# A two-layer hybrid backbone: where the low part of u is formed, and where the latent gates' modulation sums are taken

## The chip, the core and the metric

The kernel runs on one core of a Trainium2 chip. The metric is the device time of one execution in microseconds. The core's engines are TensorE (PE, matrix products; PEld is its weight load), VectorE (DVE), ScalarE (ACT), GpSimd (POOL) and SyncE (SP, which issues nearly all transfers here). Each engine works through its own queue in order; they meet through semaphores. TensorE reads SBUF and writes PSUM; VectorE and ScalarE read both.

## The reference, cut to what matters

```python
def conformer_conv(va, vg, p):
    u = va * jax.nn.sigmoid(vg)
    u = depthwise_conv(u, p["conv_w"], p["conv_b"], CONV_PAD)        # 31 taps
    return jax.nn.silu(layernorm(u, p["ln_g"], p["ln_b"]))

def rglru_branch(xb, p, h0, with_outputs):
    u = depthwise_conv(xb, p["sconv_w"], p["sconv_b"], SHORT_CONV_PAD)   # 4 taps
    # gates r, i = sigmoid(per-head products of u); a = exp(-8 r softplus(-lam))
    # b = sqrt(1 - a^2) * i * u; scan h = a h + b forward and backward
    ...

def even_mixer(h, h0, p):
    va, vg, ga, xb, gb = jnp.split(h @ p["w_in"], ...)
    y_a = conformer_conv(va, vg, p) * jax.nn.silu(ga)
    y_b = rglru_branch(xb, p, h0, True) * jax.nn.silu(gb)
    return jnp.concatenate([y_a, y_b], axis=-1) @ p["w_out"]

# layer: shift, scale, gate = split(silu(c) @ mod_w + mod_b, 3)
#        x = x + gate * mixer(rmsnorm(x) * (1 + scale) + shift)
# layer 0 is even_mixer; layer 1 is a pooling mixer; a final rmsnorm follows.
```

There are 1024 latent tokens and 256 context tokens of width 1024. The context passes only through the RG-LRU branch and gives the states with which the latent scans start.

## The kernel before

All values are kept transposed: 128 features on the partitions, tokens along the free dimension. A 1024-wide operand is `KT = 8` tiles. Products are made in three passes: each operand is split into a high part rounded to fp32r (a cast on ScalarE, L95) and a low part (the difference, on VectorE or GpSimd, L96), and high·high, high·low and low·high are added in PSUM (L126 to L128, and L508 to L510 for the gates).

The first stage, to about 90 us, loads x and the context, takes the modulation's sums for shift and scale, normalises, and folds weights of the second layer. A modulation sum (`mod_tile`, L212 and L216) multiplies a 128 x 1024 tile of weights by the vector silu(c) and adds along the row.

Then come eight rounds, j = 0 to 7, one for each 128 features of both branches. In round j:

- `uc` is the short convolution of `xb` (ScalarE L531, VectorE L534), `uh` and `ul` its high and low part. `ul` is made by `split` on VectorE as soon as `uc` and `uh` are there.
- `decays(j-1)` turns the gates of the round before into the scan's factors, on ScalarE (L449, a chain kept in order, with three changes of the activation table).
- The products `vg` (sigmoid on ScalarE, `sg`) and `va` follow; `u = va * sg` is made in two halves on VectorE (L564, called `va_0` and `va_1` here), with raised priority.
- `recurrence(j-1)`: GpSimd multiplies (L463, then a pair L465, one for each direction), VectorE multiplies (L468), scans the context (L475) and the latents (L477) for each direction, and adds both (L480).
- `project_xb(j+1)` makes the next round's `xb`, and the gate products of round j (`gate_steps`) are woven into it. The first pass of a gate product needs `uh`, the second `ul`.

In the last round there is no next `xb`; the gate products are woven into `va`. The 31 taps of the long convolution (L739, one tensor in PSUM, one in SBUF) run on VectorE whenever it is free, through the rounds and after them. GpSimd also makes the low parts of the weights (`wl_xb`, `wl_gw` and so on), and adds the layer norm's sums (`lnsum`, L748 and L751).

After the rounds come the products `gb` (silu on ScalarE L719, multiplied with the scan's result on VectorE L720, split again) and `wob` (taken out of PSUM by VectorE L789 with the latent gate `m0`), the layer norm (`mu`, `ms_ln`), `ga`, the rest of layer 0, and layer 1. Before the `gb` products the eight modulation sums of the latent gate (tiles 16 to 23) are loaded and taken, two for each of the first four `gb` steps, from a freshly loaded copy `cG` of silu(c).

The order of the work on each engine is set by a scheduler: it simulates the program as written, with priorities (`tc.high_priority`) and explicit orders (`tc.issue_after`), and writes one fixed queue for each engine. PSUM tiles of products come from four buffers in turn (`pm`): in a round they are `vg_0`, `vg_1`, `va_0`, `va_1`, the context part of the next `xb`, and then the gate groups, so that the second gate group takes the buffer of `va_0` and the third that of `va_1`. Wide tiles of a round (`utile`, `ltile`) come from pools of four and six buffers.

Of the kernel before, what the change touches and what calls it, by code (L numbers as in the profile page):

```python
# [15 lines left out]
P = 128  # L16
# [39 lines left out]
def body(ctx, tc, xT, ctxT, cc, ccol, modT, modW, win, gw, wout, wu, grp, wg, wo1, small, edge, ident, outT):  # L56
# [37 lines left out]
    def split(src, hi, lo, eng):  # L94
        return (nc.scalar.copy(hi, src),  # L95
                eng.tensor_tensor(out=lo, in0=src, in1=hi.bitcast(F32), op=sub))  # L96
# [12 lines left out]
    def wload(src, name, eng, n=D, out=None):  # L109
        raw = wpool.tile([P, n], F32, tag="wr", name=f"wr_{name}")  # L110
        load(raw, src)
        if out is None:
            hi = wpool.tile([P, n], F32R, tag="wh", name=f"wh_{name}")
            lo = wpool.tile([P, n], F32R, tag="wl", name=f"wl_{name}")
        else:
            hi, lo = out(f"wh_{name}", F32R), out(f"wl_{name}", F32R)
        split(raw, hi, lo, eng)
        return hi, lo
# [311 lines left out]
    with ExitStack() as actx:  # L430
# [84 lines left out]
        def weave(some, others, n):  # L515
            for _ in some:
                for _ in range(n):
                    next(others, None)
            for _ in others:
                pass  # L520
# [5 lines left out]
        for j in range(KT):  # L526
            uc = utile(f"uc{j}")

            for src, dst in zip(xb, (uc[:, :C], uc[:, C:])):
                n = src.shape[-1]  # L530
                nc.scalar.activation(dst, src, AF.Identity, bias=col(O_SCB + j), scale=col(O_SCW + 4 * j + 2))  # L531
                for k, o in ((0, -2), (1, -1), (3, 1)):
                    a, b = max(0, -o), n - max(0, o)
                    nc.vector.scalar_tensor_tensor(out=dst[:, a:b], in0=src[:, a + o : b + o],  # L534
                                                   scalar=col(O_SCW + 4 * j + k), in1=dst[:, a:b],
                                                   op0=mult, op1=add)
            uh, ul = utile(f"uh{j}", F32R), utile(f"ul{j}", F32R)
            split(uc, uh, ul, nc.vector)

            roots, root = (None, None) if state is None else decays(j - 1, state[1])  # L540
            w = wload(win[KT + j], f"vg{j}", nc.gpsimd)
            sg = []
            for h in range(2):
                ps = psum(f"vg{j}_{h}")
                mm3(ps, w, (hh, hl), HALF[h])
                t = ttile(f"sg{j}_{h}")
                with ExitStack() as octx:
                    if root is not None:
                        octx.enter_context(tc.issue_after(root.ins))
                    octx.enter_context(tc.high_priority(offset=EVAC))  # L550
                    nc.scalar.activation(t, ps, AF.Sigmoid)
                sg.append(t)
            w = wload(win[j], f"va{j}", nc.gpsimd)
            u = xtile(f"u{j}")
            us.append(u)
            gates, last = [], j == KT - 1
            gate = lambda: gate_steps(j, wload(gw[j], f"gw{j}", nc.gpsimd, n=4 * P), (uh, ul), gates)

            def value_steps():
                for h in range(2):  # L560
                    ps = psum(f"va{j}_{h}")
                    yield from mm3_steps(ps, w, (hh, hl), HALF[h])
                    with tc.high_priority(offset=EVAC):
                        nc.vector.tensor_tensor(out=u[:, HALF[h]], in0=ps, in1=sg[h], op=mult)  # L564

            weave(gate() if last else (), value_steps(), 1)
            if state is not None:
                recurrence(j - 1, *state, roots)
            if not last:
                xb, steps = project_xb(j + 1)  # L570
                weave(gate(), steps, 2)
            state = uc, gates
        recurrence(KT - 1, *state, decays(KT - 1, state[1])[0])

# [4 lines left out]
    def d2tile(name, dt=F32):  # L579
        return d2pool.tile([P, S], dt, tag="d2", name=name)  # L580
# [120 lines left out]


    bh, bl = [], []
    cG = d2tile("cG")
    load_c(0, cG)
    for j in range(KT):
        for m in range(2 * KT + 2 * j, min(2 * KT + 2 * j + 2, 3 * KT)):
            raw = d2tile(f"mod0_{m}")
            nc.sync.dma_start(raw, modT[0, m])
            mod_tile(m0, 0, m, raw, (cG,), raw)  # L710
        w = wload(win[4 * KT + j], f"gb{j}", nc.gpsimd)
        th, tl = d2tile(f"ybh{j}", F32R), d2tile(f"ybl{j}", F32R)
        for h in range(2):
            ps = psum(f"gb{j}_{h}")
            mm3(ps, w, (hh, hl), HALF[h])
            y = vtile(f"yr{j}_{h}")
            nc.sync.dma_start(y, yb_raw[j][:, HALF[h]])
            sgt = ttile(f"sb{j}_{h}")
            nc.scalar.activation(sgt, ps, AF.Silu)  # L719
            nc.vector.tensor_tensor(out=y, in0=y, in1=sgt, op=mult)  # L720
            split(y, th[:, HALF[h]], tl[:, HALF[h]], nc.gpsimd)
        bh.append(th)
        bl.append(tl)
# [701 lines left out]
```

## Time and profile before

| | |
|---|---|
| median of 3 runs (lowest to highest) | 1399.46 us (1398.16 to 1401.67) |
| the profiled execution: its time, its span | 1398.43 us, 1396.7 us |
| busy: TensorE, VectorE, ScalarE, GpSimd | 1299.7, 1192.6, 635.9, 362.3 us |
| mean granted TensorE clock | 0.97 |
| first stage; rounds 1 to 6; last round | to 92; 148 to 444; 444 to 484 us |
| `gb` and `wob`; `ga`; the rest | 484 to 678; 678 to 766; 766 to 1397 us |

Busy time of one engine lies beside that of others, so it is no sum. What can be gained is the time in which the engine that sets the end of a stage stands still, and that is read from that stage's waits. In rows of instructions the columns are: start, duration, engine, line, operation, tiles written and read, shape, count, and in brackets the idle time before and what ended it. In rows of waits they are: who, for whom, us in total, times, longest.

### The profile page before, as it was taken

The numbers are of one execution on the slowest core, as the hardware profiler recorded it, in microseconds if no ns is written. First come the engines' busy times: TensorE is split into PE (matmuls) and PEld (weight loads), VectorE is DVE, ScalarE is ACT, GpSimd is POOL, SyncE is SP. The second block draws the span as 40 slices with busy tenths as digits, with TensorE's granted clock in tenths as the row PEclk, the third lists the DMA queues.
The fourth block names the chain that finished last, engine by engine and source line by source line (L and its number), as shares of the span: only waits on it lengthen the run. The fifth ranks groups of instructions, "written<-read, shape, count | busy, mean of one in ns | idle before, by whom it ended". The sixth has DMA issues, their size and how long they took to land.

```text
span 1396.7 us, 15641 instructions
## 1 busy us (share of the span) xinstructions
PE 1299.7 (93%) x5664; PEld 1053.0 (75%) x5664; DVE 1192.6 (85%) x1587; ACT 635.9 (46%) x909; POOL 362.3 (26%) x182
## 2 busy tenths in 40 slices
PE   7889989898899799989999899999999999999895
PEld 4468877787777587868888688788878888778684
DVE  7984898999889999988888974999989987876675
ACT  6353653664474542311643544654333434634442
POOL 5182633652464453522521004100000000000002
PEclk9999999999999899999999999999999999999998
DMA  9741111111102116343344636523334334757623
GB/s 358 269 136 39 45 46 46 53 39 60 53 23 77 46 52 241 106 153 126 127 139 167 211 121 203 159 83 134 137 121 143 114 112 130 263 189 271 203 106 121
DMA packets 83010, 182.32 MB, mean 131 GB/s; under 512 B 7794, under 2 KB 27634, under 8 KB 82932
## 3 DMA queue, kind: packets, MB, share of 16 engines
q1 hardware_dynamic: 74484, 177.12, 36.7%
q10 hardware_dynamic: 8448, 4.20, 1.0%
q8 instruction: 44, 0.72, 0.2%
q14 instruction: 34, 0.28, 0.1%
HBM read 137.25 MB, written 44.04 MB: 130 GB/s over the span
## 4 chain that ended last, share of the span: by engine, by line
PE 53%; DVE 29%; DMA 6%; issue 6%; ACT 4%; POOL 1%; SPq 0%; DVEq 0%; POOLq 0%; ACTq 0%
DVE conv L739 7%; DVE g L468 2%; DVE g L477 2%; PE wob L126 2%; PE wob L128 2%; PE wob L127 2%; DVE junk L212 1%; PE fold L251 1%; PE vg L126 1%; PE vg L128 1%; PE fold L250 1%; DMA yr_t<-y_t 1%; PE xb L126 1%; PE xb L127 1%; PE fold L249 1%
## 5 line engine op out<-in xcount | busy, mean ns | idle before, releaser
L739 DVE SCALAR_TENSOR_TENSOR conv<-u,sm,conv 128x1021 f32<-128x1021 f32 (+14 forms) x232 | 292.1, 1272 | 6.5 <-ACT conv L731 3.8
L1245 POOL TENSOR_TENSOR o<-x,rr 128x256 f32<-128x256 f32 (+1 forms) x9 | 8.3, 942 | 462.5 <-ACT rr L1233 460.3
L511 ACT ACTIVATE g<-g,sm 128x512 f32<-128x512 f32 (+1 forms) x96 | 58.7, 617 | 126.5 <-PE g L510 124.3
L463 POOL TENSOR_TENSOR g<-g,uc 128x1280 f32<-128x1280 f32 x16 | 48.3, 3017 | 125.0 <-ACT g L511 78.9
L96 POOL TENSOR_TENSOR wl_wu<-wr_wu,wh_wu 128x1024 fp32r<-128x1024 f32 x16 | 38.7, 2421 | 153.6 <-ACT wh_wu L95 148.2
L508 PE MATMUL g<-uh,wh_gw 128*128 128x512 f32 (+1 forms) x96 | 37.0, 386 | 29.5 <-DVE u L564 22.2
L249 PE MATMUL fold<-gh,wh_wu 128*128 128x512 f32 x128 | 52.5, 411 | 4.6 <-ACT wh_wu L95 4.6
L126 PE MATMUL wob<-ybh,wh_wob 128*128 128x512 f32 x128 | 51.2, 404 | 5.0 <-DVE xp L789 4.9
L250 PE MATMUL fold<-gl,wh_wu 128*128 128x512 f32 x128 | 51.7, 404 | 3.7 <-DVE gl L96 3.7
L128 PE MATMUL xb<-h0h,wl_xb 128*128 128x512 f32 x128 | 50.8, 396 | 4.2 <-POOL wl_xb L96 4.2
L126 PE MATMUL gb<-h0h,wh_gb 128*128 128x512 f32 x128 | 51.4, 402 | 3.4 <-ACT sb L719 3.3
L251 PE MATMUL fold<-gh,wl_wu 128*128 128x512 f32 x128 | 51.2, 409 | 2.7 <-POOL wl_wu L96 2.7
L128 PE MATMUL gb<-h0h,wl_gb 128*128 128x512 f32 x128 | 50.9, 399 | 1.6 <-POOL wl_gb L96 1.6
L126 PE MATMUL va<-h0h,wh_va 128*128 128x512 f32 x128 | 50.6, 396 | 0.8 <-ACT g L511 0.8
L126 PE MATMUL vg<-h0h,wh_vg 128*128 128x512 f32 x128 | 50.5, 395 | 0.8
L465 POOL TENSOR_TENSOR g<-g,th 128x1280 f32<-128x1280 f32 x16 | 46.9, 2953 | 16.8 <-ACT th L449 16.8
L127 PE MATMUL wob<-ybl,wh_wob 128*128 128x512 f32 x128 | 50.9, 401 | 0.0
L126 PE MATMUL xb<-h0h,wh_xb 128*128 128x512 f32 x128 | 50.9, 398 | 0.0
L127 PE MATMUL gb<-h0l,wh_gb 128*128 128x512 f32 x128 | 50.9, 397 | 0.0
L127 PE MATMUL xb<-h0l,wh_xb 128*128 128x512 f32 x128 | 50.7, 396 | 0.0
L128 PE MATMUL wob<-ybh,wl_wob 128*128 128x512 f32 x128 | 50.7, 401 | 0.0
L127 PE MATMUL va<-h0l,wh_va 128*128 128x512 f32 x128 | 50.4, 394 | 0.0
(551 smaller groups left out, 4297.9 us busy)
## 6 DMA issues: line engine op xcount, KB each, us to landing
mod<-modT SPq DMA_DIRECT2D x28, 512.0 KB, 5.9
wr_wu<-wu SPq DMA_DIRECT2D x16, 512.0 KB, 4.2
x_part<-xp SPq DMA_DIRECT2D x32, 256.0 KB, 2.4
mod<-modT SPq DMA_DIRECT2D x32, 256.0 KB, 3.4
wr_v<-wfold SPq DMA_DIRECT2D x16, 512.0 KB, 3.6
wr_g<-wg SPq DMA_DIRECT2D x16, 512.0 KB, 4.8
wr_wo<-wo SPq DMA_DIRECT2D x16, 512.0 KB, 4.4
yr_t<-y_t SPq DMA_DIRECT2D x16, 512.0 KB, 6.4
```

The lines of the kernel that those rows point to most:

```text
L96: eng.tensor_tensor(out=lo, in0=src, in1=hi.bitcast(F32), op=sub))
L126: nc.tensor.matmul(ps, hi[:, kc], xh[k][:, cols], start=(k == 0), stop=False)
L127: nc.tensor.matmul(ps, hi[:, kc], xl[k][:, cols], start=False, stop=False)
L128: nc.tensor.matmul(ps, lo[:, kc], xh[k][:, cols], start=False, stop=(k == ks - 1))
L249: nc.tensor.matmul(ps, wh[:, kc], gh[i], start=(i == 0), stop=False)
L250: nc.tensor.matmul(ps, wh[:, kc], gl[i], start=False, stop=False)
L251: nc.tensor.matmul(ps, wl[:, kc], gh[i], start=False, stop=(i == 3))
L463: nc.gpsimd.tensor_tensor(out=ius[d], in0=ius[d], in1=uc, op=mult)
L465: nc.gpsimd.tensor_tensor(out=ius[d], in0=ius[d], in1=roots[d], op=mult)
L508: nc.tensor.matmul(ps[:, :n], gwh[:, kc], uh[:, a : a + n], start=True, stop=False)
L511: nc.scalar.activation(t[:, a : a + n], ps[:, :n], AF.Sigmoid, bias=col(ob + d * KT + j))
L739: nc.vector.scalar_tensor_tensor(out=(us[j] if k == 30 else acp)[:, a:b], in0=us[j][:, a + o : b + o], scalar=col(O_CONVW + 31 * j + k), i ...
```

## The change

`ul` is no longer made by `split` in front of the round's products. In rounds 0 to 6 it is issued after the first value product has been multiplied out; in round 7 it is issued ahead of the woven `va` and gate products. The eight modulation sums of the latent gate move to round 0; they use the vector `cL`, which is still there from the first stage, and the wide buffers of the rounds, and the load and SiLU of `cG` go. The gate weights of the last round are requested in a statement ahead of `ul` and the value's steps.

```diff
             uh, ul = utile(f"uh{j}", F32R), utile(f"ul{j}", F32R)
-            split(uc, uh, ul, nc.vector)
+            nc.scalar.copy(uh, uc)
+            taken = []
...
-            gate = lambda: gate_steps(j, wload(gw[j], f"gw{j}", nc.gpsimd, n=4 * P), (uh, ul), gates)
 
             def value_steps():
                 for h in range(2):
                     ps = psum(f"va{j}_{h}")
                     yield from mm3_steps(ps, w, (hh, hl), HALF[h])
                     with tc.high_priority(offset=EVAC):
-                        nc.vector.tensor_tensor(out=u[:, HALF[h]], in0=ps, in1=sg[h], op=mult)
-
-            weave(gate() if last else (), value_steps(), 1)
+                        taken.append(nc.vector.tensor_tensor(out=u[:, HALF[h]], in0=ps, in1=sg[h], op=mult))
+
+            gws = wload(gw[j], f"gw{j}", nc.gpsimd, n=4 * P) if last else None
+            with ExitStack() as octx:
+                if not last:
+                    weave((), value_steps(), 1)
+                    octx.enter_context(tc.issue_after(taken[0].ins))
+                nc.vector.tensor_tensor(out=ul, in0=uc, in1=uh.bitcast(F32), op=sub)
+            if last:
+                weave(gate_steps(j, gws, (uh, ul), gates), value_steps(), 1)
+            if j == 0:
+                for m in range(2 * KT, 3 * KT):
+                    raw = ltile(f"mod0_{m}")[:, :D]
+                    nc.sync.dma_start(raw, modT[0, m])
+                    mod_tile(m0, 0, m, raw, (cL,), raw)
             if state is not None:
                 recurrence(j - 1, *state, roots)
             if not last:
                 xb, steps = project_xb(j + 1)
-                weave(gate(), steps, 2)
+                gws = wload(gw[j], f"gw{j}", nc.gpsimd, n=4 * P)
+                weave(gate_steps(j, gws, (uh, ul), gates), steps, 2)
...
     bh, bl = [], []
-    cG = d2tile("cG")
-    load_c(0, cG)
     for j in range(KT):
-        for m in range(2 * KT + 2 * j, min(2 * KT + 2 * j + 2, 3 * KT)):
-            raw = d2tile(f"mod0_{m}")
-            nc.sync.dma_start(raw, modT[0, m])
-            mod_tile(m0, 0, m, raw, (cG,), raw)
         w = wload(win[4 * KT + j], f"gb{j}", nc.gpsimd)
```

What the scheduler makes of it is seen in the queues. VectorE in round 1, before (`g_0_1` and `g_1_1` are the scan's inputs of the two directions, `conv` rows are taps of the long convolution, the two L564 rows are `va_0` and `va_1`):

```order
L96 TENSOR_TENSOR ul_1191<-uc_1181,uh_1190 128x1280
...
L468 SCALAR_TENSOR_TENSOR g_0_1_1079<-g_0_0_1045,g_0_1_1079 128x1280
...
L468 SCALAR_TENSOR_TENSOR g_1_1_1147<-g_1_0_1113,g_1_1_1147 128x1280
L564 TENSOR_TENSOR u_1268<-va_0_1269,sg_0_1233 128x512
L475 SCALAR_TENSOR_TENSOR g_0_1_1079<-g_0_0_1045,g_0_1_1079 128x256
L739 SCALAR_TENSOR_TENSOR conv_3862<-u_978,sm,conv_3862 128x1017
L475 SCALAR_TENSOR_TENSOR g_1_1_1147<-g_1_0_1113,g_1_1_1147 128x256
L477 SCALAR_TENSOR_TENSOR g_0_1_1079<-g_0_0_1045,g_0_1_1079 128x1024
L739 SCALAR_TENSOR_TENSOR conv_3862<-u_978,sm,conv_3862 128x1016
L477 SCALAR_TENSOR_TENSOR g_1_1_1147<-g_1_0_1113,g_1_1_1147 128x1024
L564 TENSOR_TENSOR u_1268<-va_1_1295,sg_1_1260 128x512
```

The same place now:

```order
L468 SCALAR_TENSOR_TENSOR g_0_1_1111<-g_0_0_1077,g_0_1_1111 128x1280
L746 SCALAR_TENSOR_TENSOR conv_3859<-u_977,sm,conv_3859 128x1018
L475 SCALAR_TENSOR_TENSOR g_0_1_1111<-g_0_0_1077,g_0_1_1111 128x256
L468 SCALAR_TENSOR_TENSOR g_1_1_1179<-g_1_0_1145,g_1_1_1179 128x1280
L564 TENSOR_TENSOR u_1299<-va_0_1300,sg_0_1264 128x512
L571 TENSOR_TENSOR ul_1223<-uc_1213,uh_1222 128x1280
L746 SCALAR_TENSOR_TENSOR conv_3859<-u_977,sm,conv_3859 128x1017
L477 SCALAR_TENSOR_TENSOR g_0_1_1111<-g_0_0_1077,g_0_1_1111 128x1024
L475 SCALAR_TENSOR_TENSOR g_1_1_1179<-g_1_0_1145,g_1_1_1179 128x256
L746 SCALAR_TENSOR_TENSOR conv_3859<-u_977,sm,conv_3859 128x1016
L564 TENSOR_TENSOR u_1299<-va_1_1326,sg_1_1291 128x512
```

`ul` has moved from the front to just behind `va_0`, and the second direction's long scan (L477) from ahead of `va_1` to behind it. (Taps have line 746 in the changed kernel.)

VectorE in round 3, before:

```order
L96 TENSOR_TENSOR ul_1795<-uc_1785,uh_1794 128x1280
L745 COPY u_1268<-conv_3895 128x15
L468 SCALAR_TENSOR_TENSOR g_0_1_1683<-g_0_0_1649,g_0_1_1683 128x1280
L739 SCALAR_TENSOR_TENSOR conv_3930<-u_1570,sm,conv_3930 128x1009
L475 SCALAR_TENSOR_TENSOR g_0_1_1683<-g_0_0_1649,g_0_1_1683 128x256
L468 SCALAR_TENSOR_TENSOR g_1_1_1751<-g_1_0_1717,g_1_1_1751 128x1280
L564 TENSOR_TENSOR u_1872<-va_0_1873,sg_0_1837 128x512
L739 SCALAR_TENSOR_TENSOR conv_3930<-u_1570,sm,conv_3930 128x1010
L477 SCALAR_TENSOR_TENSOR g_0_1_1683<-g_0_0_1649,g_0_1_1683 128x1024
L475 SCALAR_TENSOR_TENSOR g_1_1_1751<-g_1_0_1717,g_1_1_1751 128x256
L739 SCALAR_TENSOR_TENSOR conv_3930<-u_1570,sm,conv_3930 128x1011
L564 TENSOR_TENSOR u_1872<-va_1_1899,sg_1_1864 128x512
```

And now:

```order
L468 SCALAR_TENSOR_TENSOR g_0_1_1715<-g_0_0_1681,g_0_1_1715 128x1280
L475 SCALAR_TENSOR_TENSOR g_0_1_1715<-g_0_0_1681,g_0_1_1715 128x256
L746 SCALAR_TENSOR_TENSOR conv_3927<-u_1601,sm,conv_3927 128x1009
L477 SCALAR_TENSOR_TENSOR g_0_1_1715<-g_0_0_1681,g_0_1_1715 128x1024
L468 SCALAR_TENSOR_TENSOR g_1_1_1783<-g_1_0_1749,g_1_1_1783 128x1280
L746 SCALAR_TENSOR_TENSOR conv_3927<-u_1601,sm,conv_3927 128x1010
L564 TENSOR_TENSOR u_1903<-va_0_1904,sg_0_1868 128x512
L571 TENSOR_TENSOR ul_1827<-uc_1817,uh_1826 128x1280
L475 SCALAR_TENSOR_TENSOR g_1_1_1783<-g_1_0_1749,g_1_1_1783 128x256
L746 SCALAR_TENSOR_TENSOR conv_3927<-u_1601,sm,conv_3927 128x1011
L564 TENSOR_TENSOR u_1903<-va_1_1930,sg_1_1895 128x512
```

Here the first direction's long scan has moved ahead of the second L468, of `va_0` and of `ul`. Round 6 reads like round 3 in the changed kernel.

SyncE, which issues the loads, in round 0, before:

```order
L105 DMA wr_va_972<-win 128x1024
L255 DMA wfold_82<-fo_3_0_791 128x4x128
L255 DMA wfold_82<-fo_3_1_807 128x4x128
L105 DMA wr_xb_1031<-win 128x1024
L105 DMA wr_gw_1039<-gw 128x512
L105 DMA wr_vg_1202<-win 128x1024
```

And now:

```order
L105 DMA wr_xb_1063<-win 128x1024
L577 DMA mod_16_1031<-modT 128x1024
L577 DMA mod_17_1035<-modT 128x1024
L577 DMA mod_18_1039<-modT 128x1024
L577 DMA mod_19_1043<-modT 128x1024
L577 DMA mod_20_1047<-modT 128x1024
L577 DMA mod_21_1051<-modT 128x1024
L577 DMA mod_22_1055<-modT 128x1024
L577 DMA mod_23_1059<-modT 128x1024
L105 DMA wr_gw_1071<-gw 128x512
L105 DMA wr_vg_1233<-win 128x1024
```

The eight loads of modulation weights stand between the weights of `xb` and of the gates. On VectorE their sums stand in round 0 among the taps of the short convolution and ahead of `va_0`. TensorE's order in rounds 0 to 6 is the same in both kernels. In round 7, ScalarE, SyncE and GpSimd hold the gate weights at the same places as before, and TensorE has the first gate product's second pass right behind its first, where a few passes of `va` stood between them. After round 7, the order of the `gb` and `wob` steps differs in detail: the `wob` products stand half after half instead of mixed, and `mu` stands behind 252 of them instead of 282.

## The prediction

> **What bounds the kernel now.** I read the page's busy shares first, then TensorE's waits over the whole run, then the length and granted clock of each round, then one round instruction by instruction.
>
> ```profile
> span 1396.7 us, 15641 instructions
> PE g L508 <- DVE u L564: 22.2, 6, 5.2
> PE g L508 <- ACT wh_gw L95: 6.4, 1, 6.4
> PE wob L126 <- DVE xp L789: 4.9, 2, 2.7
> PE xb L128 <- POOL wl_xb L96: 4.2, 2, 2.9
> PE gb L126 <- ACT sb L719: 3.3, 1, 3.3
> DVE ul L96 <- ACT uh L95: 24.3, 7, 5.9
> ```
>
> TensorE is the engine that sets the end: it is busy for most of the span, and these are its largest waits after the first stage (total, times, longest). The first is the one that the change aims at. In rounds 1 to 6 the third group of gate products needs the PSUM buffer of the second value product (`va_1`), and VectorE multiplies that buffer out late. The last row is VectorE's own wait: it stands at the head of its queue for `ul`, which needs `uh` from ScalarE.
>
> The six rounds, cut at the first `vg` product of rounds 1 to 7 (columns: length; busy time of PE, PEld, DVE, ACT, POOL; granted clock, DMA share, GB/s), and TensorE's waits in the third of them:
>
> ```profile
> 148.30:198.30 50.00, 44.64 (x206) 37.10 (x205) 43.35 (x37) 27.00 (x32) 21.52 (x9) 0.97 0.14 48
> 198.30:245.95 47.65, 44.52 (x205) 37.13 (x204) 43.24 (x36) 25.93 (x31) 21.48 (x9) 0.96 0.14 50
> 245.95:294.10 48.15, 43.66 (x205) 35.74 (x204) 45.86 (x38) 28.30 (x34) 27.93 (x11) 1.00 0.15 50
> 294.10:344.20 50.10, 44.87 (x205) 37.87 (x204) 48.43 (x40) 26.01 (x30) 22.65 (x10) 0.93 0.14 47
> 344.20:395.20 51.00, 45.63 (x206) 37.91 (x205) 45.96 (x38) 26.11 (x31) 21.68 (x9) 0.93 0.13 47
> 395.20:444.50 49.30, 44.94 (x206) 36.83 (x205) 42.92 (x36) 27.05 (x32) 26.85 (x11) 0.97 0.18 59
> PE g L508 <- DVE u L564: 2.2, 1, 2.2
> PE xb L128 <- POOL wl_xb L96: 1.3, 1, 1.3
> PE g L508 <- DVE uc L534: 0.9, 1, 0.9
> ```
>
> Round 3 ran at clock 1.00 and waited 4.4 us, so a round without waits takes 48.15 − 4.4 = 43.8 us. The six took 296.2, that is 33.4 us over 6 × 43.8. The waits explain 22.2 + 4.2 + 0.9 = 27.3 of it; the other 6.1 are products at the lower clock, which stands in the rounds whose wait was about 3 us or more. VectorE is nearly as full as TensorE (269.8 of 296.2 us), so there is at most 26.4 us in these rounds whatever is moved.
>
> Round 1 on VectorE, GpSimd and TensorE:
>
> ```profile
> 164.59 3.02 DVE L96 TENSOR_TENSOR ul<-uc,uh 128x1280 fp32r<-128x1280 f32 x1 [4.69 <-ACT uh L95]
> 168.72 2.50 DVE L468 SCALAR_TENSOR_TENSOR g<-g,g 128x1280 f32<-128x1280 f32 x1
> 172.33 1.58 DVE L468 SCALAR_TENSOR_TENSOR g<-g,g 128x1280 f32<-128x1280 f32 x1
> 174.43 0.67 DVE L475 TENSOR_TENSOR_SCAN g<-g,g 128x256 f32<-128x256 f32 x1
> 179.04 1.25 DVE L739 SCALAR_TENSOR_TENSOR conv<-u,sm,conv 128x1016 f32<-128x1016 f32 x1
> 180.20 2.34 DVE L477 TENSOR_TENSOR_SCAN g<-g,g 128x1024 f32<-128x1024 f32 x1
> 182.46 0.66 DVE L564 TENSOR_TENSOR u<-va,sg 128x512 f32<-128x512 f32 x1
> 160.38 5.88 POOL L465 TENSOR_TENSOR g<-g,th 128x1280 f32<-128x1280 f32 x2 [1.93 <-ACT th L449]
> 166.21 3.66 POOL L96 TENSOR_TENSOR wl_xb<-wr_xb,wh_xb 128x1024 fp32r<-128x1024 f32 x1
> 171.26 1.30 POOL L96 TENSOR_TENSOR wl_gw<-wr_gw,wh_gw 128x512 fp32r<-128x512 f32 x1 [1.39 <-DVE g L468]
> 175.42 0.28 PE L509 MATMUL g<-ul,wh_gw 128*128 128x256 f32 x1
> 183.18 0.79 PE L508 MATMUL g<-uh,wh_gw 128*128 128x512 f32 x1 [5.23 <-DVE u L564]
> ```
>
> Two things are to be seen. First, TensorE stopped at 183.18 − 5.23 = 177.95, and the product that it needs ended at 183.12. Second, a VectorE instruction with two SBUF tensors and a GpSimd instruction never run together: `ul` starts at 164.59 and lasts 3.02, but GpSimd's pair ends at 166.26, so its own time is 1.35; `wl_xb` behind it ends at 169.87, 2.26 after `ul` did; the first L468 ends at 171.22, again 1.35 after that. The convolution taps (one PSUM tensor) show no such wait. [...]
>
> **The change, part by part.** (1) `ul` behind the first value product, rounds 1, 2, 4, 5. The order is then L468, tap, scan, L468, `va_0`, `ul`, tap, long scan, short scan, tap, `va_1`. Worked for round 1 with the own times above. The first L468 needs the first half of GpSimd's pair (done at 163.3), but the second half starts at once, so it runs from 166.26 to 167.6. `wl_xb` takes GpSimd to 169.9. The tap lies beside it; the short scan (0.6) ends at 170.5, the second L468 at 171.9, `va_0` (0.6) at 172.5. `wl_gw` runs 171.9 to 173.2, `ul` to 174.6. Tap (1.2) 175.8, long scan (2.3) 178.0, short scan 178.6, tap 179.8, `va_1` 180.4. TensorE waits 2.5 instead of 5.23. It uses `ul` first at 175.42, so 174.6 is just in time. The gain over before comes from VectorE's idle 4.69 and from one long scan that now stands behind `va_1`; what takes the idle's place is the wait for the GpSimd pair. Rounds 2 and 5 have the same order, round 4 one tap earlier (1.9). A wait of 2.5 may or may not be followed by the lower clock: round 3's 2.2 was not, round 2 and round 6 with 2.9 to 3.0 were; I add 0.7 each (half of the 1.0 to 2.0 that it costs).
>
> (2) Rounds 3 and 6, where GpSimd also adds up the layer norm's sums and the first long scan now stands ahead of `ul`:
>
> ```profile
> 263.83 2.55 POOL L748 TENSOR_TENSOR lnsum<-u,u 128x512 f32<-128x512 f32 x1
> 413.06 5.04 POOL L751 TENSOR_TENSOR lnsum<-lnsum,u 128x512 f32<-128x512 f32 x2
> ```
>
> Round 3 by the same rule, from the pair's end at 263.9: L468 265.3, `lnsum` 266.4, short scan 267.0, `wl_xb` 269.3, long scan 271.6, `lnsum` 272.7, L468 274.1, tap 275.3, `va_0` 275.9, `ul` 277.3. TensorE wants `ul` 2.5 us ahead of its third group, about 274.0 here, so it now waits 3.3 on `ul` itself, a wait that the kernel before does not have, and 0.6 on `wl_xb`. With 0.9 for `uc` and 1.0 of lower clock the round is 5.8 over 43.8, where it was 4.35. Round 6 (two `lnsum` ahead of `wl_xb`) comes to about 6.5 where it was 5.5; two instructions want GpSimd's place there within 0.1 us, so it may be 5.6 or 7.
>
> Sum of (1) and (2): 3.2 + 3.2 + 5.8 + 2.4 + 3.2 + 6.5 = 24.3 over the floor instead of 33.4: **9 us gained**. Lower end 4 (all waits followed by the lower clock, both ties lost); upper end 26.4 (VectorE's busy time). I take 9, because both ends leave out something that the rows show. [...]
>
> (3) Last round. The queues of ScalarE, SyncE and GpSimd hold the gate weights where they were, so nothing is moved ahead there; only TensorE now has the product with `ul` right behind the first one.
>
> ```profile
> 461.71 0.60 ACT L95 CAST wh_gw<-wr_gw 128x512 fp32r<-128x512 f32 x1
> 456.50 5.75 POOL L465 TENSOR_TENSOR g<-g,th 128x1280 f32<-128x1280 f32 x2 [1.93 <-ACT th L449]
> 460.70 2.90 DVE L96 TENSOR_TENSOR ul<-uc,uh 128x1280 fp32r<-128x1280 f32 x1 [1.32 <-ACT uh L95]
> ```
>
> The 6.4 us wait for `wh_gw` stays, since it ends a chain on ScalarE that starts with the gates of the round before. `ul` ends at 463.6 behind GpSimd's pair, 0.9 after TensorE wants it: **1 us lost** (0 to 1).
>
> (4) The modulation sums in round 0, and their absence later:
>
> ```profile
> L212 DVE SCALAR_TENSOR_TENSOR mod<-mod,cG 128x1024 f32<-128x1024 f32 x8 | 10.2, 1271 | 0.0
> L216 DVE TENSOR_TENSOR m<-m,sm 128x1 f32<-128x1 f32 x8 | 3.1, 392 | 0.0
> 544.19 0.62 ACT L95 CAST ybh<-yr 128x512 fp32r<-128x512 f32 x1 [8.62 <-DVE yr L720]
> mod<-modT SPq DMA_DIRECT2D x12, 512.0 KB, 7.6
> 113.82 0.34 SPq L105 DMA_DIRECT2D wr_gw<-gw  x1
> 0.00:90.00 90.00, 70.06 (x253) 45.78 (x254) 81.66 (x137) 47.33 (x72) 44.02 (x27) 0.96 0.75 274
> 122.83 0.69 DVE L564 TENSOR_TENSOR u<-va,sg 128x512 f32<-128x512 f32 x1 [6.47 <-PE va L128]
> ```
>
> In the gb and wob stage VectorE loses 13.3 us of work, ScalarE a load's wait and the SiLU of `cG`, SyncE nine loads. TensorE's waits there were 3.3 (ScalarE's `sb`, behind a cast that waited 8.62 for VectorE) and 4.9 (`xp`): together 8.2, less than the 13.3, so they should go. Against that TensorE reaches `mu` 30 products sooner in its order, some 7 us, and may wait for the sums. I take **7 us gained**; ends 0 (VectorE's relief used up by the earlier arrival) and 12 (the slow clock behind those waits goes too).
>
> In round 0 the sums fill VectorE's idle (6.47 us before `va_0`, and what lies ahead of it). The eight loads stand ahead of `wr_gw` on SyncE, and the last two need the buffers of the first two sums. From about 96 us, with 7.6 us to landing when the queues were full, the last lands near 120; the sums end near 122, where `va_0` begins at 122.83. TensorE needs that product only for the third group of gate products, some 10 us later. Cost 0; if the cover is gone, see the rival.
>
> Sum: 9 − 1 + 7 = 15 us off the profiled execution's 1398.4, which stands 1.0 under the median of the runs: **1383 us**. Behind the wob stage TensorE has few waits, and every engine it meets there is fed by the same stages, so I carry the 15 to the end unchanged.
>
> **The rivals.** *The lock does not bind* (the first L468 gets in between GpSimd's two multiplications): every step of (1) is 2.6 to 3 us earlier and the waits vanish, 26 in the rounds, 7 behind: 1366. For it, VectorE's idle of 24.3; against it, each contended row above. [...] *The later stage gives nothing*: `mu` arrives early or `yr` stays late, and rounds 3 and 6 lose their ties: 4 to 8 gained, 1392. For it, both waits that I count there are waits for VectorE, directly or through ScalarE, and it has no slack of its own that I have shown. *No change that counts*: the time regained in the rounds is lost at `ul` in rounds 3 and 6 and at `mu`: 1396. *Slower*: the loads of round 0 land one after another at 7.6 us each. Then the last sum ends at about 96 + 8 × 7.6 = 157 us instead of 122, `va_0` stands behind it on VectorE, TensorE's third gate group (about 133) waits 24 us, and the gain of 15 turns into 9 lost: 1407. It decides once the last sum ends later than 148; against it, the first stage moved 274 GB/s (the row of its window), 1.9 us for one such load when many are under way.
>
> **How the numbers follow.** Forecast 0.55 (own range 1376 to 1389), lock does not bind 0.13, later stage gives nothing 0.17, no change that counts 0.09, slower 0.06. The range 1368 to 1397 takes in the forecast, the third and the fourth, and half of the second; what it leaves out is about 0.15. About 0.3% (4 us) is what a measurement can tell from no change here; faster by more than that is 0.55 + 0.13 + 0.17 = 0.85, within it 0.09, slower 0.06.
>
> **What would show it.** TensorE's wait on L564 falls from 22.2 to about 10, VectorE's wait of `ul` for `uh` goes, and the first L468 of a round lasts about 4 us or is idle until GpSimd's pair ends. L509 waits for `ul` in rounds 3 and 6, about 3 us each, and 1 us in round 7; `wh_gw` still costs 6 us. The waits on `sb` and `xp` go. The forecast is wrong if the sums of round 0 delay `va_0`, if the six rounds end less than 4 or more than 15 us sooner, or if `mu` waits over 5 us.

## The result, and the profile after

| | before | changed |
|---|---|---|
| median (lowest to highest), us | 1398.81 (1392.68 to 1401.67) | 1376.73 (1375.11 to 1381.07) |
| the profiled execution: its time, its span, us | 1398.43, 1396.7 | 1381.07, 1379.3 |

The ratio is 0.9853, with an interval of 0.9812 to 0.9894: 15 to 26 us gained (22 between the medians), where 15 was forecast. The profiled execution of the changed kernel is the slowest of the four, 4.3 us above their median; so a second profile of it, from the run `after_again` below (span 1373.9 us, median 1377.07 us), is read beside the first. Of `last_only` below only the times are read, since its profiled execution ran at a granted clock of 0.65.

TensorE's waits in rounds 1 to 6 of the changed kernel, then in the last round, then from the first `gb` product to the first `qc_woa` product of layer 1 (who, for whom, us in total, times, longest):

```profile
PE g L508 <- DVE u L564: 6.2, 3, 2.3
PE g L509 <- DVE ul L571: 6.0, 2, 3.0
PE g L508 <- ACT g L511: 2.5, 2, 1.9
PE vg L126 <- ACT g L511: 2.1, 4, 0.7
PE xb L128 <- POOL wl_xb L96: 2.0, 2, 1.6
...
PE g L508 <- ACT wh_gw L95: 6.4, 1, 6.4
PE g L509 <- DVE ul L571: 0.7, 1, 0.7
...
PE gb L128 <- POOL wl_gb L96: 4.8, 2, 3.3
PE wob L127 <- POOL ybl L96: 1.2, 2, 0.9
PE wob L128 <- POOL wl_wob L96: 0.7, 1, 0.7
```

The wait for `va_1` fell from 22.2 to 6.2, a wait for `ul` of 3.0 came in two rounds, `wh_gw` is unchanged, and `sb` and `xp` are gone. New in the rounds, and in no forecast, are 4.6 us of waits for ScalarE to take gate products out of PSUM (the two rows of `g` L511). The same stretches as whole windows (rounds 1 to 6, last round, `gb` to `qc_woa`, the rest; length first, then busy times, clock, DMA), before, then changed:

```profile
148.33:444.46 296.13, 268.19 (x1226) 222.54 (x1224) 269.74 (x220) 160.33 (x185) 142.04 (x55) 0.96 0.15 50
444.46:483.90 39.44, 32.05 (x133) 24.81 (x131) 37.94 (x30) 25.41 (x32) 18.32 (x7) 0.91 0.10 34
483.90:772.90 289.00, 274.99 (x1173) 223.43 (x1173) 258.14 (x345) 102.32 (x136) 106.18 (x54) 0.98 0.40 137
772.90:1396.70 623.80, 596.13 (x2598) 487.05 (x2598) 510.20 (x828) 278.43 (x460) 28.82 (x25) 0.97 0.46 158
```
```profile
149.56:436.52 286.96, 267.65 (x1225) 220.05 (x1224) 276.09 (x219) 159.85 (x185) 143.44 (x55) 0.97 0.16 52
436.52:476.40 39.88, 32.49 (x134) 25.49 (x132) 37.78 (x30) 25.58 (x32) 17.51 (x8) 0.87 0.11 33
476.40:756.30 279.90, 270.82 (x1172) 220.82 (x1172) 250.56 (x322) 99.88 (x133) 105.92 (x54) 0.99 0.38 125
756.30:1379.30 623.00, 595.31 (x2598) 485.83 (x2598) 509.89 (x828) 277.80 (x460) 28.65 (x25) 0.98 0.47 158
```

So 9.2 us came from rounds 1 to 6, 9.1 from the stretch behind the last round, 0.8 from the rest; the last round lost 0.4 and the work ahead of round 1 1.2. In the second profile the four windows are 284.0, 39.9, 280.1 and 621.6, and round 1 begins at 148.32, as before the change.

Round 1 of the changed kernel on VectorE and GpSimd, beside the row by row forecast:

```profile
164.59 4.24 DVE L468 SCALAR_TENSOR_TENSOR g<-g,g 128x1280 f32<-128x1280 f32 x1 [2.14 <-POOL g L465]
169.94 1.70 DVE L475 TENSOR_TENSOR_SCAN g<-g,g 128x256 f32<-128x256 f32 x1
171.56 1.46 DVE L468 SCALAR_TENSOR_TENSOR g<-g,g 128x1280 f32<-128x1280 f32 x1
173.54 1.97 DVE L571 TENSOR_TENSOR ul<-uc,uh 128x1280 fp32r<-128x1280 f32 x1
180.63 0.68 DVE L564 TENSOR_TENSOR u<-va,sg 128x512 f32<-128x512 f32 x1
161.61 5.87 POOL L465 TENSOR_TENSOR g<-g,th 128x1280 f32<-128x1280 f32 x2 [1.92 <-ACT th L449]
167.44 3.65 POOL L96 TENSOR_TENSOR wl_xb<-wr_xb,wh_xb 128x1024 fp32r<-128x1024 f32 x1
```

The first L468 was released when half of GpSimd's pair was done, and then ran 4.24 us, until 1.35 after the pair's end at 167.48. A tap, which has one tensor in PSUM, took 1.27 beside `wl_xb` (L746 at 168.75) and 1.27 with GpSimd idle (at 175.44). The L564 row is `va_1`; it ends at 181.31, 13.8 behind the pair's end (forecast 14.1).

### The profile page after: what moved, and what is told of

It is laid out like the page before. It is cut to its first block, busy times and chain, and to the rows that moved or that the text cites. A ratio compares the mean times of both kernels' runs of the same rounds, so it can differ in the third digit from the quotient of the medians.

```text
span 1379.3 us, 15637 instructions
## 1 busy us (share of the span) xinstructions
PE 1295.9 (94%) x5664; PEld 1048.2 (76%) x5664; DVE 1205.1 (87%) x1587; ACT 632.7 (46%) x906; POOL 363.3 (26%) x182
## 4 chain that ended last, share of the span: by engine, by line
PE 36%; DVE 10%; DMA 7%; issue 2%; ACT 2%; POOL 1%; POOLq 0%; SPq 0%; DVEq 0%; ACTq 0%
PE ga L127 2%; PE ga L128 2%; PE ga L126 2%; PE wob L127 2%; PE wob L128 2%; PE wob L126 2%; DMA wr_g<-wg 1%; DVE ws L986 1%; DMA yr_t<-y_t 1%; DMA wr_v<-wfold 1%; PE qb_g L666 1%; DVE wq_g L96 1%; PE qb_g L669 1%; PE qb_g L668 1%; DVE wq_wo L96 1%
## 5 line engine op out<-in xcount | busy, mean ns | idle before, releaser
L746 DVE SCALAR_TENSOR_TENSOR conv<-u,sm,conv 128x1013 f32<-128x1013 f32 (+14 forms) x232 | 291.2, 1272 | 6.6 <-ACT conv L738 3.8
L511 ACT ACTIVATE g<-g,sm 128x512 f32<-128x512 f32 (+1 forms) x96 | 58.8, 617 | 110.5 <-PE g L510 108.3
L96 POOL TENSOR_TENSOR wl_wu<-wr_wu,wh_wu 128x1024 fp32r<-128x1024 f32 x16 | 39.4, 2470 | 153.9 <-ACT wh_wu L95 147.7
L465 POOL TENSOR_TENSOR g<-g,th 128x1280 f32<-128x1280 f32 x16 | 46.9, 2948 | 16.8 <-ACT th L449 16.8
L127 PE MATMUL vg<-h0l,wh_vg 128*128 128x512 f32 x128 | 51.2, 400 | 0.0
L128 PE MATMUL va<-h0h,wl_va 128*128 128x512 f32 x128 | 50.4, 395 | 0.0
```

Source lines behind the costliest of these rows:

```text
L127: nc.tensor.matmul(ps, hi[:, kc], xl[k][:, cols], start=False, stop=False)
L128: nc.tensor.matmul(ps, lo[:, kc], xh[k][:, cols], start=False, stop=(k == ks - 1))
L465: nc.gpsimd.tensor_tensor(out=ius[d], in0=ius[d], in1=roots[d], op=mult)
L511: nc.scalar.activation(t[:, a : a + n], ps[:, :n], AF.Sigmoid, bias=col(ob + d * KT + j))
L746: nc.vector.scalar_tensor_tensor(out=(us[j] if k == 30 else acp)[:, a:b], in0=us[j][:, a + o : b + o], scalar=col(O_CONVW + 31 * j + k), i ...
```

## The experiments

Each table cell of time is in us; the rounds are windows 1 to 6 as above, "stretch" is `gb` to `qc_woa`.

| run | median | ratio to before (95% interval) | rounds 1 to 6 | last round | stretch |
|---|---|---|---|---|---|
| `after_again` | 1377.07 | 0.9856 (0.9830 to 0.9882) | 284.0 | 39.9 | 280.1 |
| `ul_only` | 1390.00 | 0.9934 (0.9912 to 0.9955) | 284.9 | 39.9 | 292.0 |
| `mods_only` | 1390.85 | 0.9949 (0.9929 to 0.9968) | 298.3 | 39.5 | 281.0 |
| `last_only` | 1399.33 | 1.0002 (0.9986 to 1.0018) | not read | not read | not read |
| `extra` | 1396.69 | 0.9995 (0.9979 to 1.0011) | 299.7 | 41.1 | 282.7 |
| `scan_late` | 1371.57 | 0.9804 (0.9784 to 0.9824) | 281.6 | 37.0 | 280.2 |
| `value_first` | 1381.74 | 0.9877 (0.9856 to 0.9898) | 282.1 | 37.0 | 286.9 |
| `both` | 1372.82 | 0.9817 (0.9798 to 0.9837) | 278.6 | 35.5 | 284.8 |
| `loads_again` | 1382.11 | 0.9885 (0.9864 to 0.9906) | 283.1 | 39.4 | 287.1 |
| `pair_vector` | 1383.83 | 0.9900 (0.9880 to 0.9920) | 279.6 | 38.9 | 291.9 |
| `pair_scan` | 1377.58 | 0.9857 (0.9832 to 0.9882) | 276.3 | 39.6 | 291.8 |
| `sums_again` | 1558.55 | 1.1148 (1.1127 to 1.1169) | 305.0 | 48.9 | 433.9 |

### The three parts by themselves

The first four share their runs of the kernel before.

> The changed kernel once more, beside its parts. From the first profile of it: rounds 1 to 6 take 287 us (296 before), the last round 40 (39), gb with wob to the first ga product 187 (194), the rest as before; ratio to the kernel before 0.985 (0.981 to 0.989). Either theory below expects this.

`ul_only` has the changed `ul` in rounds 0 to 6, with the sums and the last round of the kernel before:

```diff
-            gws = wload(gw[j], f"gw{j}", nc.gpsimd, n=4 * P) if last else None
...
+            if last:
+                gws = wload(gw[j], f"gw{j}", nc.gpsimd, n=4 * P)
+                weave(gate_steps(j, gws, (uh, ul), gates), value_steps(), 1)
+            else:
+                weave((), value_steps(), 1)
+                with tc.issue_after(taken[0].ins):
+                    nc.vector.tensor_tensor(out=ul, in0=uc, in1=uh.bitcast(F32), op=sub)
```

> Only the move of ul in rounds 0 to 6; the modulation sums stay with the gb products and the last round is that of the kernel before. Theory A (the parts add up, each in its own stage): rounds 1 to 6 at 287 us, gb with wob at 194 as before, ratio 0.9935 (9 us gained). Rival B (VectorE must finish the same work before the layer norm, so what the rounds gain without the sums' removal is lost again at gb and wob): rounds 287, gb with wob 199 to 203, ratio 0.997 to 1.000.

`mods_only` is the kernel before with the sums in round 0:

```diff
+            if j == 0:
+                for m in range(2 * KT, 3 * KT):
+                    raw = ltile(f"mod0_{m}")[:, :D]
...
-    cG = d2tile("cG")
-    load_c(0, cG)
```

> Only the eight modulation sums move to round 0; ul and the last round are those of the kernel before. Theory A: round 0 costs nothing, rounds 1 to 6 stay at 296 us, gb with wob falls from 194 to 187, the waits on sb and xp go; ratio 0.995. Rival B (the relief counts only when the rounds are shorter too): gb with wob 192 to 194, ratio 0.999 to 1.000. Rival C (the sums delay the first value product in round 0): round 0 longer than 45.3 us by 1 us or more.

`last_only` is the kernel before with the last round's statements:

```diff
+            if last:
+                gws = wload(gw[j], f"gw{j}", nc.gpsimd, n=4 * P)
+                nc.vector.tensor_tensor(out=ul, in0=uc, in1=uh.bitcast(F32), op=sub)
+                weave(gate_steps(j, gws, (uh, ul), gates), value_steps(), 1)
```

> Only the last round's part: the gate weights requested in a statement ahead of ul, and ul ahead of the woven products. The order of the gate weights in the queues of ScalarE, SyncE and GpSimd is the same, so theory A expects the wait of 6.4 us for wh_gw to stay and a ratio of 1.000 (within 0.3%). Rival: the statement's place does bring the gate weights ahead of what holds them: the wait falls to 1 to 3 us, 3 to 5 us gained, ratio 0.997.

All three ratios are those of theory A. Multiplied, 0.9934 × 0.9949 × 1.0002 is 0.9885, where the whole is 0.9856: some 4 us less than the whole gained. The intervals of the four ratios are too wide to tell this from an exact sum. The windows show where such a difference can come from. `ul_only` gained 11 in the rounds and gave 3 back in the stretch (292.0 where 289.0 stood), mostly at one wait, 3.3 us in the kernel before:

```profile
PE gb L126 <- ACT sb L729: 7.8, 1, 7.8
```

That is a part of rival B, of half the size that B named. `mods_only` gained 8 in the stretch; the two together come to 5 there, where the whole gained 9. In `mods_only` round 0 kept its 45.28 us, so rival C falls.

### Is it the exclusion that leaves 2 us in each round?

`extra` adds one GpSimd instruction behind the pair that nobody reads:

```diff
-                nc.gpsimd.tensor_tensor(out=ius[d], in0=ius[d], in1=roots[d], op=mult)
+                pair = nc.gpsimd.tensor_tensor(out=ius[d], in0=ius[d], in1=roots[d], op=mult)
+            if j < KT - 2:
+                with tc.issue_after(pair.ins):
+                    nc.gpsimd.tensor_tensor(out=cL, in0=uc[:, :D], in1=uc[:, :D], op=mult)
```

> The changed kernel with one more GpSimd multiplication in each of rounds 1 to 6, 128 x 1024, directly behind the pair L465; nobody reads its result, and it holds no buffer that the path waits for. Theory A (a VectorE instruction with two SBUF tensors and a GpSimd instruction exclude each other): the extra 2.3 us push the second L468, ul, the scans and va_1 back too, so TensorE's waits on L564 and on ul stay at 2 to 3 us a round on top of wl_xb being 2.3 us later: rounds 1 to 6 take 14 to 17 us more (301 to 304). Rival D (no exclusion; GpSimd's instructions only delay their own queue): wl_xb comes 2.3 us later, VectorE's steps stay where they are, and the wait on L564 shrinks by what TensorE loses at wl_xb: rounds 1 to 6 take 5 to 9 us more, the waits on L564 and ul fall below 5 in sum, and the second L468 stays at 1.5 us.

VectorE's two L468 of round 1 and GpSimd beside them, then TensorE's waits over the run:

```profile
163.20 4.24 DVE L471 SCALAR_TENSOR_TENSOR g<-g,g 128x1280 f32<-128x1280 f32 x1 [2.13 <-POOL g L465]
169.66 3.59 DVE L471 SCALAR_TENSOR_TENSOR g<-g,g 128x1280 f32<-128x1280 f32 x1
166.04 3.15 POOL L468 TENSOR_TENSOR cL<-uc 128x1024 f32<-128x1024 f32 x1
169.16 2.75 POOL L96 TENSOR_TENSOR wl_xb<-wr_xb,wh_xb 128x1024 fp32r<-128x1024 f32 x1
```
```profile
PE g L511 <- DVE u L567: 17.2, 5, 7.8
PE xb L128 <- POOL wl_xb L96: 4.6, 4, 2.2
```

L468 is the added instruction in this file, and the L468 of the other files is L471. VectorE's second one went from 1.46 to 3.59 us with nothing changed in its data; it ended 1.34 us after `wl_xb` did, which is about its own time. The waits for `va_1` rose to 17.2 on top of those for `wl_xb`. The rounds took 299.7, 13 to 16 more than the two profiles of the changed kernel: at the lower end of theory A's range and above rival D's, and D had expected the second one to stay at 1.5. One GpSimd instruction per round, whose result nobody reads, cost 19.6 us in the median, about as much as the whole change gains.

`pair_vector` moves the pair (L465) to VectorE, and `pair_scan` adds to it the later scans of the next section:

```diff
-                nc.gpsimd.tensor_tensor(out=ius[d], in0=ius[d], in1=roots[d], op=mult)
+                nc.vector.tensor_tensor(out=ius[d], in0=ius[d], in1=roots[d], op=mult)
```

> The changed kernel with the pair L465 on VectorE instead of GpSimd. Theory A (the two engines exclude each other, so GpSimd's 5.9 us for the pair are 5.9 us in which VectorE can do only taps): VectorE does the pair in 2.7 us in place of 2.1 us idle and 2.8 us inside the first L468; va_1 and ul come 2 to 3 us sooner in rounds 1 to 6, the waits on L564 (about 6 to 8) and ul (6) mostly go, rounds 1 to 6 at 276 to 280 us where the changed kernel had 284 and 287, ratio 0.977 to 0.982. Rival H (VectorE is simply full, 274.6 of 284 us, and 16 us of added work bind): rounds 1 to 6 at 288 or more, ratio 0.988 or above.

> The pair L465 on VectorE and both long scans behind va_1, together. In the run with the late scans alone, the waits on L564 and ul went and waits of 2.1 us for the short convolution of the next round (uc) came in rounds 1, 3 and 6. Theory A: VectorE is 2 to 3 us ahead in every round, so these go too: rounds 1 to 6 at 270 to 275 us (floor 263), ratio 0.973 to 0.977. If the work ahead of mu binds after the rounds, mu or xp waits of 3 us or more take back part of it and the ratio is 0.978 to 0.981.

In the rounds rival H falls: they took 279.6 and 276.3, though VectorE took over 12 multiplications. The first length is in theory A's range, the second just above it (270 to 275). But the waits that theory A named did not go. In `pair_vector` those on L564 (9.5) and `ul` (4.0) came to 13.5 in the rounds, against 14.5 in the second profile of the changed kernel. In round 1 the wait for `va_1` fell from 2.2 to 0.6, while in round 3 VectorE now has both long scans ahead of `va_1`:

```profile
178.40 0.50 PE L508 MATMUL g<-uh,wh_gw 128*128 128x512 f32 x1 [0.62 <-DVE u L564]
273.34 0.79 PE L508 MATMUL g<-uh,wh_gw 128*128 128x512 f32 x1 [4.03 <-DVE u L564]
```

What the rounds gained came from the waits for ScalarE (3.8) and for `wl_xb` (2.0), which went. In `pair_scan` 7.8 us of waits for `uc` stayed. So the pair on GpSimd is shown to hold up `va_1` in round 1; for the other rounds the run gives no answer, since the order changed with it.

The ratios, 0.9900 and 0.9857, are worse than theory A's (the first is rival H's, the second lies above both ranges), because of one wait, the same in both (that of `pair_vector`):

```profile
PE ga L126 <- DVE u L838: 11.5, 1, 11.5
```

VectorE comes out of the rounds with the added work still in its queue as taps of the long convolution (113 of them lie in the rounds, where the changed kernel has 123), and the layer norm's multiplication of `u` (L838) is late for `ga`. The rounds and the stretch share one sum of VectorE's work: what does not fit into the rounds must be finished before `ga`.

### The waits that were left

`scan_late` puts both long scans behind `va_1` (`before` is `taken[1]` in rounds 1 to 6, and nothing in the last round):

```diff
+                with ExitStack() as octx:
+                    if before is not None:
+                        octx.enter_context(tc.issue_after(before.ins))
+                    nc.vector.tensor_tensor_scan(out=iu[:, lat], data0=at[:, lat], data1=iu[:, lat],
+                                                 initial=first, op0=mult, op1=add)
```

> The changed kernel with both long scans (L477) behind va_1 in rounds 1 to 6. Theory A (the waits that are left are VectorE's work ahead of va_1 and ul): 2.3 us less stand ahead of va_1 in rounds 1, 2, 4, 5 and 2.3 us less ahead of ul in rounds 3 and 6; the waits on L564 (6.2) go, those on ul fall from 6.7 to 2 to 3, rounds 1 to 6 at 276 to 280 us, 7 to 10 us gained on the changed kernel, ratio to the kernel before 0.977 to 0.980. Rival E (the later scans hold buffers or work that TensorE meets elsewhere in the round): new waits of the same size at the gate groups, rounds 1 to 6 within 3 us of 287.

```profile
PE g L511 <- DVE uc L537: 7.7, 5, 2.2
...
PE g L511 <- ACT wh_gw L95: 4.3, 1, 4.3
```

The waits for `va_1` went and those for `ul` fell to 0.4 in the rounds, as theory A said; but 7.7 us of waits for the next round's short convolution came in their place (rival E: the same VectorE work, later). The rounds gained 2 to 5, not 7 to 10, and the last round 3, with 4.3 for `wh_gw` instead of 6.4. The gain in the rounds is hardly clear of the spread: `ul_only`, `value_first` and `loads_again` have VectorE's order of the changed kernel in rounds 1 to 6 and took 284.9, 282.1 and 283.1 there. With 0.9804 it is the lowest ratio of all (that of `both` lies within its interval), about 0.5% under the changed kernel.

`value_first` takes 36 of `va`'s 48 products ahead of the first gate product in the last round, and `both` joins it with the later scans:

```diff
-                weave(gate_steps(j, gws, (uh, ul), gates), value_steps(), 1)
+                steps = value_steps()
+                for _ in range(12):
+                    next(steps)
+                weave(gate_steps(j, gws, (uh, ul), gates), steps, 1)
```

> The changed kernel, with 36 of the 48 products of va in the last round ahead of the first gate product (now three of its passes meet the gate weights first). Theory A (the wait of 6.4 us is a matter of TensorE's own order; the gate weights come at 454.4 whatever stands ahead): the wait falls to below 1 us and the one on ul (0.7) goes, last round 33 to 35 us instead of 40, 5 to 6 us gained. Rival F: the gate groups now stand back to back, ScalarE takes them out at 0.7 us each and TensorE waits there, so that less than 3 us is gained.

> The long scans behind va_1 and va first in the last round, together. If both theories hold, 12 to 16 us gained on the changed kernel: ratio to the kernel before 0.973 to 0.977. If the gain of the rounds is lost later since VectorE must still finish the same work before the layer norm: mu or xp waits of 3 us or more and a ratio above 0.980.

The last round's one wait in `value_first`:

```profile
PE g L508 <- DVE u L564: 5.5, 1, 5.5
```

The wait for `wh_gw` is gone and a wait for a value product to be taken out of PSUM by VectorE stands in its place: the size is rival F's (2.9 gained in the last round), the cause is not the one F named. The stretch was 7 longer, with 5.1 of waits for ScalarE's cast `wq_woa` and 3.1 for `ybh` that the changed kernel does not have there; `mu` now stands behind 285 `wob` products there instead of 252, and whether that order is the cause was not tried. `both` kept the gain of `scan_late` and no more.

### What did the move of the sums gain from?

`loads_again` issues the eight loads a second time where they stood before; `sums_again` does VectorE's part there a second time, without loads:

```diff
+        for m in range(2 * KT + 2 * j, min(2 * KT + 2 * j + 2, 3 * KT)):
+            raw = d2tile(f"again0_{m}")
+            nc.sync.dma_start(raw, modT[0, m])
```
```diff
+        for m in range(2 * j, min(2 * j + 2, KT)):
+            junk = d2tile(f"again0_{m}")
+            with tc.issue_after(taken.ins):
+                nc.vector.scalar_tensor_tensor(out=junk, in0=us[0], scalar=1.0, in1=us[0], ...)
```

> The changed kernel with the eight 512 KB loads of the latent gate's modulation weights issued a second time where they stood before the change, two ahead of each of the first four gb steps; nothing reads them there and no sum is taken there. Theory A (gb and wob gained 6 to 7 us since VectorE has 13.3 us less to do): gb with wob stays at 187 us, ratio to the kernel before 0.9856 as for the changed kernel. Rival G (the gain comes from the transfers that are gone: SyncE's queue and the yr and gb weight loads behind them): gb with wob back at 192 to 194, ratio 0.989 to 0.991.

> The changed kernel with VectorE's part of the latent gate's sums done a second time, without any transfer: two products with a sum along the row and two small adds behind each of the first four gb steps, on the finished u of the first round, into tiles that nobody reads (13.3 us of VectorE work, as before the change). The run with the loads alone gave back 5 us. Theory A (VectorE's work is what the gb and wob stages gained from): the stretch from the first gb product to the first qc_woa product goes from 280 us (changed kernel) back to 286 to 290, ratio 0.989 to 0.991. Theory G (the transfers are): the stretch stays at 279 to 282, ratio 0.984 to 0.987. If both count, the two runs together give back more than the 7 us that the move gained.

With the loads alone the stretch gave back 7 of its 9 us (287.1), and the median 5; the ratio, 0.9885, is nearer rival G's. TensorE's waits there, and what ScalarE waited for (11.7 in the changed kernel):

```profile
PE wob L126 <- ACT ybh L95: 4.1, 1, 4.1
PE gb L126 <- ACT wh_gb L95: 3.8, 1, 3.8
...
ACT cH L225 <- DMA cH<-cc: 16.7, 1, 16.7
```

ScalarE stands 5 us longer at `cH`, which has two of the extra loads ahead of it in SyncE's queue. The cast of `wh_gb` is queued behind that and behind a cast of `ybh`, which needs VectorE's first product `yr`. That product's place differs too; VectorE in `loads_again`, then in the second profile of the changed kernel:

```profile
514.15 13.12 DVE L749 SCALAR_TENSOR_TENSOR conv<-u,sm,conv 128x1023 f32<-128x1023 f32 x11
527.86 1.37 DVE L730 TENSOR_TENSOR yr<-yr,sb 128x512 f32<-128x512 f32 x2 [0.58 <-DMA yr<-yb_raw]
```
```profile
514.03 8.39 DVE L746 SCALAR_TENSOR_TENSOR conv<-u,sm,conv 128x1023 f32<-128x1023 f32 x7
```

Eleven taps stand ahead of `yr` where seven stood, and VectorE still waited 0.58 for the load of `yr` behind them: here the transfer came last. The wait on `ybh` was not followed further. TensorE has `mu` behind 250 `wob` products here, close to the 252 of the changed kernel. But the waits that the change had removed, `sb` and `xp`, did not come back: the run shows that eight loads in this place cost some 5 us, with the order that the scheduler makes of them, and not that the change gained its 9 by their absence. `sums_again` answers nothing: its order differs already in the rounds, where the taps that fill VectorE stand 16 times instead of 123 (rows of the taps in rounds 1 to 6, then TensorE's largest wait):

```profile
149.58:454.59 305.01, 20.36 (x16) 0.95 0.15 49
...
PE mu L779 <- DVE lnsum L764: 110.9, 1, 110.9
```

What VectorE's 13.3 us are worth by themselves, and so how the gain of the stretch divides, stays open.

## Why the prediction was right, point by point

**Rounds.** Forecast 24.3 over the floor of 262.8, so 9 gained; the first profile has 24.2 (9.2 gained), the second 21.2, and `ul` alone 22.1. The waits of `va_1` were forecast at 2.5, 2.5, 1.9, 2.5 in rounds 1, 2, 4, 5 and came as 2.2, 2.2 or none, 1.7, 2.3; `ul` in rounds 3 and 6 at 3.3 and came at 3.0; `wl_xb` at 0.6 and came at 0.4. The replay by "VectorE's instruction starts when GpSimd's ends" was good to half a microsecond for each of these waits but the one in round 2 that is missing in the first profile. For the length of a round it was not: rounds 1 and 3 were forecast at 47.0 and 49.6 and took 48.45 and 48.46 in the first profile. The sum lacked the waits for ScalarE (4.6 in the first profile, 3.8 in the second), had 0.9 for `uc`, which did not come, and 9.4 for `va_1`, of which 6.2 came in the first profile and 8.4 in the second; that 24.3 met 24.2 so closely is partly luck.

**A term that was right in some rounds only is the lower clock, added on top of the waits** (0.5 to 1.0 a round; for round 4 the sum has 0.5 where its text says 0.7). Round 2 shows where it was wrong (first profile, then the second):

```profile
198.01:244.12 46.11, 45.87 (x204) 37.94 (x205) 44.20 (x36) 26.64 (x31) 22.12 (x9) 0.93 0.15 52
```
```profile
196.76:242.88 46.12, 43.18 (x204) 35.92 (x205) 44.20 (x36) 26.66 (x31) 22.56 (x9) 1.00 0.16 52
PE g L508 <- DVE u L564: 2.2, 1, 2.2
```

Once TensorE ran at 0.93 and did not wait for `va_1`, once it ran at 1.00 and waited 2.2: the round took 46.1 both times. The slow clock stood at the round's start (0.66 in its first 10 us), ahead of the wait, and was paid out of it. Round 5 is the other case:

```profile
339.23:386.88 47.65, 44.66 (x205) 37.30 (x205) 46.97 (x38) 26.66 (x31) 22.62 (x9) 0.96 0.15 50
```
```profile
336.47:382.61 46.14, 43.14 (x205) 35.91 (x205) 45.50 (x37) 26.66 (x31) 22.62 (x9) 1.00 0.16 52
```

The wait for `va_1` was 2.27 both times. Behind it the clock was 0.79 for 8 us in the first profile and 1.00 in the second, and the round took 1.5 us more. So here the lower clock was added, since it fell behind the round's last wait for VectorE.

**Last round.** Forecast 1 lost; 0.4 to 0.5 lost, with `ul` at 0.7 and `wh_gw` still at 6.4. `last_only` measured no difference.

**Behind the rounds.** Forecast 7 gained; 9 in the stretch, and `mods_only` gained 8 there. The waits on `sb` and `xp` (8.2 together) went, as forecast, and no wait for `mu` came, though it stands 30 products earlier. But the kernel before had another wait in the stretch, which went too and which the sum did not have:

```profile
PE qc_woa L653 <- ACT wq_woa L95: 4.1, 1, 4.1
```

Against that the waits for GpSimd (`wl_gb`, `ybl`, `wl_wob`) rose from 1.6 to 6.7, and TensorE's busy time fell by 4.2 (274.99 to 270.82, nearly the same count of products at clock 0.99 instead of 0.98), which the prediction had kept for its upper end. So the size is in part luck. The reason given, VectorE's 13.3 us, is not shown; the runs that were to decide between it and the loads left it open.

**Round 0.** Forecast no cost; 45.28 us before and after. The last sum ended at 125.97, not 122, and `va_0` came at 126.08, 2 us later than before when the round's own later start (1.2) is taken off:

```profile
124.74 1.21 DVE L212 SCALAR_TENSOR_TENSOR mod<-mod,cL 128x1024 f32<-128x1024 f32 x1
125.89 0.08 DVE L212 DVE_READ_ACCUMULATOR mod<-mod,cL 128x1 f32 x1
126.08 0.69 DVE L564 TENSOR_TENSOR u<-va,sg 128x512 f32<-128x512 f32 x1
```

TensorE had no wait for it in that round. By the order of the buffers it asks for that of `va_0` at 134.69, 7.9 us after VectorE had emptied it (forecast some 10). From "slower" (a last sum at 157, harmful from 148) this was 22 us away: the loads of that rival took 7.6 us each, one after another, and these landed 4.5 to 5.9 us after their issue, beside each other.

**Rivals.** "The lock does not bind" fell (4.24 for the first L468). "The later stage gives nothing" fell (9 in the stretch), and with the two gains "no change that counts". Against its own profile the forecast was 2 us short, which is the stretch; the other 4 to the median are the spread between executions, 3 of them in the rounds of the second profile.

## What to carry to other kernels

Replay a stage row by row with the own times of its instructions and with GpSimd and VectorE taking turns as the rows showed it (3.59 us beside 1.46 for one L468): that gave the waits for both within half a microsecond, and missed those for ScalarE, which was not replayed. A slower TensorE clock cost nothing where it fell ahead of a wait for another engine (46.11 and 46.12 us in round 2) and was added where it fell behind the last one (1.5 us in round 5). Work that VectorE is given in one stage may be paid for in the next (11.5 us at `ga`). When a step is moved away, count its transfers as closely as its arithmetic: eight loads put back, without their sums, cost 5 us, and TensorE's waits name only other engines for it. A forecast can meet the total with wrong terms, so compare it wait by wait.

## What the runs showed of the hardware

The same wait was followed by different clocks. Round 1's wait for `va_1` was 2.20 us in the first profile and 2.21 in the second; the 6.9 us behind it:

```profile
181.36:188.20 6.84, 6.84 (x37) 5.99 (x38) 6.80 (x5) 2.92 (x5) 0.00 (x0) 1.00 0.19 77
```
```profile
180.12:187.00 6.88, 6.88 (x31) 6.10 (x32) 6.84 (x5) 2.31 (x4) 0.00 (x0) 0.75 0.19 76
```

The clock was 1.00 once and 0.75 the other time: a wait of 2.2 us was followed by a lower clock in one execution and by none in the other. Whether the wait brought it about was not tried.
